# A decoder layer in split fp32: the set subtractions go from GpSimd to VectorE, and the merge gates' sigmoids stand one product behind their load

## The chip, the cores and the metric

The kernel runs on one core of a Trainium2 chip. TensorE multiplies matrices, VectorE, ScalarE and GpSimd work element by element, and the queue of SyncE (SP) issues nearly all DMAs. Each engine works through its own queue in order; semaphores tie the queues together. The metric is the device time of one execution in microseconds (us). In the profile PE is TensorE (PEld its weight loads), DVE VectorE, ACT ScalarE, POOL GpSimd and SP SyncE.

## The reference

One layer over 2048 rows of width 1024, float32:

```python
u = x * (1.0 + scale) + shift                    # scale, shift, gate from silu(c) @ w_ada
q, k, v, a_gate, p_in, p_gate, m_a, m_p = split(u @ w_in)
a = sliding_window_sink_attention(q, k, v, ...) * silu(a_gate)
a = a @ w_attn_proj
p = einsum('bsgc,gcd->bsgd', multiscale_causal_pool(p_in), w_pool_mix)
p = (p * pool_scale) * silu(p_gate)
p = p @ w_pool_proj
y = sigmoid(m_a) * a + sigmoid(m_p) * p
y = (y @ w_out) * (1.0 + gate)
x = layer_norm(DEEPNORM_ALPHA * x + y, ln_gain, ln_bias)
```

## The kernel before

**Products.** Every float32 operand is split in two: a high part (a cast to the multiplier's 32-bit type, on ScalarE) and a low part (operand minus high part, on VectorE or GpSimd). One block product is three passes of four matmuls, high by high, high by low, low by high: twelve matmuls of 128x512. These twelve are the kernel's unit of time, called a product or a tick below.

**Seven products for eight.** Two tiles of 128 weight columns by two column halves of 512 rows would be eight block products; a `Quad` does them with seven by a Strassen-Winograd scheme. It needs sums of weight blocks, made on GpSimd per quad (`sum1`, line 268; `mid`, 272 and 273; `late`, 277), and sums of the other operand's blocks. These latter, the *sets*, are named B11, T1, T2, B21, T3, B22, T4; they are made once per stage and then serve all quads of it. `pair_split` (lines 305 and 131: cast, then low part) splits a quad's weight blocks into `w_set` tiles, three times per quad.

**Where the sets come from.** `sums_to` (line 198) makes a later stage's sets aside of the running stage: it loads four blocks into two `spare` tiles of 128x1024 (`fetch`), then does four subtractions of 128x512 in place, one after the other (`sub`: T1, T2, T4, T3, each on the result of an earlier one), and stores each result to DRAM through SP. With the first load at tick 0, the subtractions are put at ticks 4, 5.5, 7 and 8.5 and their stores 2.5 ticks behind. There are 24 such sets of four: 4 in the first stage (there with a scaling of the loaded blocks ahead, so 3.5 ticks later), 8 in the second, and 12, one each 8 ticks, in the merge part. So 96 subtractions, on GpSimd, line 212, shown in the profile as line 56, GpSimd, `spare<-spare` (some use other tiles as room, `first_qs`, `second_qs`, `second_kk`). In the stage that uses them `set_steps` loads the sets again and splits them (`set_T` and `set_B` in the profile), between the products.

**Order.** `pe`, `act`, `dve`, `pool` and `sp` are engines whose instructions keep the program's order among themselves (line 56 is this wrapper); calls by `nc.` may be put elsewhere by the scheduling layer below. `ring` runs groups of two quads; after each product it calls `tick`, which runs what hooks and `defer` have put at that tick.

**Stages.** 0 to 260 us: modulation, first sets and the gates of half the rows; 260 to 605 attention of that half, with products filling it; 605 to 800 and 800 to 1193 the same for the other half; 1193 to 1560 the merge part: for each half the attention projection and the pool projection, four times two groups; then the output product and the norm.

**The merge gates.** In the merge part each product's result is multiplied by a sigmoid. `gates_ahead` (line 594) makes `ahead`, which `back` calls when a group starts and again two ticks later: it loads four gate tiles `g` for both quads together each time (SP), and applies the sigmoid on ScalarE (line 605). The result of product B21 (tick 2 for the first quad) is the first to use one, by lines 616, 625 and 627.

Of the kernel before, what the change touches and what calls it, by code (L numbers as in the profile page):

```python
# [14 lines left out]
AF = mybir.ActivationFunctionType  # L15
ALU = mybir.AluOpType
# [43 lines left out]
def kernel(  # L60
# [22 lines left out]
    nc = tc.nc  # L83
    pe, act, dve, pool, sp = (Ordered(tc, e) for e in (nc.tensor, nc.scalar, nc.vector, nc.gpsimd, nc.sync))
# [110 lines left out]
    def put(q, store, name, i, src):  # L195
        q.dma_start(store[name][i // 2, :, i % 2, :], src)

    def sums_to(ph, store, i, load, work=None, sums=True):

        b = []  # L200

        def x(r, c):
            return b[r][:, c * CH : (c + 1) * CH]

        def fetch():
            b.extend((ph.spare(), ph.spare()))
            b.reverse()
            for r in (1, 0):
                load(b[r], r)

        def sub(out, a, c):
            return lambda: pool.tensor_tensor(x(*out), x(*a), x(*c), ALU.subtract)

        todo = [(0, fetch)]
        if work:
            todo += [(3, lambda: work(b[0], 0)), (3.5, lambda: work(b[1], 1))]
        made = [("B11", (0, 0)), ("B21", (1, 0)), ("B22", (1, 1))] if work else []
        if work and not sums:
            made.insert(1, ("B12", (0, 1)))
        puts = [(5 + 0.6 * n, *x) for n, x in enumerate(made)]  # L220
        if sums:
            at = 7.5 if work else 4
            for out, a, c, name in (
                ((0, 1), (0, 1), (0, 0), "T1"),
                ((1, 1), (1, 1), (0, 1), "T2"),
                ((1, 0), (1, 0), (1, 1), "T4"),
                ((0, 0), (1, 1), (0, 0), "T3"),
            ):
                todo.append((at, sub(out, a, c)))
                puts.append((at + 2.5, name, out))  # L230
                at += 1.5
        for at, name, z in puts:
            todo.append((at, lambda name=name, z=z: put(sp, store, name, i, x(*z))))
        return sorted(todo, key=lambda t: t[0])
# [9 lines left out]
    class Quad:  # L244
# [7 lines left out]
        def load(self, ph, own, q=nc.sync, e=nc.gpsimd):  # L252
            self.w, self.a22 = ph.weights(), ph.last(own)
            x = self.w
            if len(self.srcs[0].shape) == 3:
                for dst, src, half in ((x[:, 2, :], 1, 0), (self.a22, 1, 1), (x[:, 0, :], 0, 0), (x[:, 3, :], 0, 1)):
                    q.dma_start(dst.rearrange("p (k q) -> p k q", k=4), self.srcs[src][:, 4 * half : 4 * half + 4, :])
                if e is not None:
                    self.sum1(e)
                return  # L260
            q.dma_start(x[:, 2, :], self.srcs[1][:, 0:CH])
            q.dma_start(self.a22, self.srcs[1][:, CH:])
            q.dma_start(x[:, 0::3, :], by_two(self.srcs[0]))
            if e is not None:
                self.sum1(e)
# [186 lines left out]
    def defer(ticks, f):  # L452
        due.append((now[0] + ticks, len(due), f))
# [143 lines left out]
    def gates_ahead(name, s, m, raw):  # L597
        g = {}

        def ahead(ph, turn):  # L600
            for mi, t in (((0, 0), (1, 1)), ((0, 1), (1, 0)))[turn]:
                x = g[mi, t] = ph.c("g")
                sp.dma_start(x, gates_d[name][s, m + mi, t])
                if raw:
                    nc.scalar.activation(x, x, AF.Sigmoid)

        return g, ahead

# [1036 lines left out]
```

## Time and profile before

| | |
|---|---|
| Median of 3 runs | 1693.99 us (1690.03 to 1697.75) |
| The profiled execution's own time | 1691.31 us |
| Its span, first to last instruction | 1689.5 us |
| TensorE busy | 1647.0 us, 97% of the span |
| VectorE, ScalarE, GpSimd busy | 1204.8, 1021.7, 995.3 us |
| Granted TensorE clock, mean | 0.996 |
| Merge part, 1193 to 1560 us: TensorE, VectorE, GpSimd busy | 359.11, 314.58, 218.58 of 367 us |
| DMA share in the merge part | 0.86 |

How to read the rows. A group row gives the line, the engine, the operation, the tiles (out, then in), shapes and count; behind the first bar the busy time in us and the mean of one in ns; behind the second the engine's idle time just ahead of these instructions and what ended it. A row in order of time gives start and length in us, then the same, with the idle time ahead in brackets. A row of waits gives who waited for whom: us in total, times, longest. A row of a stretch gives, from PE to POOL, busy us and in brackets the number of instructions, then the granted TensorE clock as a share of full speed, the busy share of the DMA engines and GB/s. The shown busy time of matmuls is modelled; their pace is read from the time of twelve in a row.

### The profile page before, as it was taken

The numbers are of one execution on the slowest core, as the hardware profiler recorded it, in microseconds if no ns is written. First come the engines' busy times: TensorE is split into PE (matmuls) and PEld (weight loads), VectorE is DVE, ScalarE is ACT, GpSimd is POOL, SyncE is SP. The second block draws the span as 40 slices with busy tenths as digits, with TensorE's granted clock in tenths as the row PEclk, the third lists the DMA queues.
The fourth block names the chain that finished last, engine by engine and source line by source line (L and its number), as shares of the span: only waits on it lengthen the run. The fifth ranks groups of instructions, "written<-read, shape, count | busy, mean of one in ns | idle before, by whom it ended". The sixth has DMA issues, their size and how long they took to land.

```text
span 1689.5 us, 24673 instructions
## 1 busy us (share of the span) xinstructions
PE 1647.0 (97%) x8058; PEld 1384.2 (82%) x8058; DVE 1204.8 (71%) x2140; ACT 1021.7 (60%) x2142; POOL 995.3 (59%) x734
## 2 busy tenths in 40 slices
PE   7999999999999999999999999999999999999997
PEld 6788888888888888888788888888878877888886
DVE  6955655776857657357467677675679997989877
ACT  4644547778777756334578777776546445645452
POOL 3343347586866838762376858587567667533442
PEclk9999999999999999999999999999999999999999
DMA  9688843333423468875542334223979797878443
GB/s 360 203 260 310 212 162 107 113 126 112 150 100 107 131 233 312 271 242 181 198 138 87 126 130 136 102 93 131 325 250 392 257 372 255 323 274 280 150 150 113
DMA packets 188850, 336.80 MB, mean 199 GB/s; under 512 B 18336, under 2 KB 44080, under 8 KB 188720
## 3 DMA queue, kind: packets, MB, share of 16 engines
q1 hardware_dynamic: 185600, 330.96, 57.2%
q10 hardware_dynamic: 3088, 4.23, 1.1%
q8 instruction: 64, 1.05, 0.2%
q14 instruction: 66, 0.54, 0.1%
q0 software_dynamic: 32, 0.02, 0.0%
HBM read 227.96 MB, written 110.33 MB: 200 GB/s over the span
## 4 chain that ended last, share of the span: by engine, by line
PE 67%; DVE 12%; DMA 7%; issue 5%; ACT 5%; POOL 4%; SPq 1%; POOLq 0%; DVEq 0%; ACTq 0%
PE mm L56 44%; PE lg L56 16%; PE pv L56 4%; PE pt L56 3%; DVE w_set L131 3%; DVE set_T L56 2%; DVE set_B L56 1%; ACT L L56 1%; DMA g<-ma_d 1%; DMA g<-mp_d 1%; POOL spare L56 1%; DVE w_set L56 1%; ACT w_set L56 1%; DVE wide L627 1%; DMA W<-in_win_dram 1%
## 5 line engine op out<-in xcount | busy, mean ns | idle before, releaser
L56 PE MATMUL mm<-set_B,w_set 128*128 128x512 f32 x2664 | 655.3, 393 | 2.2 <-DVE w_set L131 1.6
L56 PEld LDWEIGHTS mm<-set_B,w_set 128*128 128x128 f32 x2664 | 497.1, 189 | 106.2 <-DVE w_set L131 3.0
L56 PE MATMUL mm<-set_T,w_set 128*128 128x512 f32 x1824 | 454.3, 395 | 6.3 <-DVE mm L56 3.9
L56 PE MATMUL lg<-set_T,w_set 128*128 128x512 f32 x1704 | 412.0, 391 | 10.1 <-DVE w_set L131 5.7
L56 PEld LDWEIGHTS mm<-set_T,w_set 128*128 128x128 f32 x1824 | 335.9, 188 | 76.5 <-DVE mm L56 6.5
L56 PEld LDWEIGHTS lg<-set_T,w_set 128*128 128x128 f32 x1704 | 319.5, 188 | 81.1 <-DVE w_set L131 6.9
L131 DVE TENSOR_TENSOR w_set<-W,w_set 128x1024 fp32r<-128x1024 f32 x138 | 203.2, 1474 | 137.6 <-ACT w_set L305 124.1
L305 ACT CAST w_set<-W 128x1024 fp32r<-128x1024 f32 x138 | 144.8, 1050 | 215.4 <-PE mm L56 134.1
L56 POOL TENSOR_TENSOR w_set<-W,w_set 128x512 fp32r<-128x512 f32 x120 | 157.3, 1319 | 116.5 <-ACT w_set L56 114.6
L268 POOL TENSOR_TENSOR W<-W,A 128x512 f32<-128x512 f32 x46 | 73.0, 1586 | 233.3 <-DMA A<-in_win_dram 66.1
L56 DVE TENSOR_TENSOR o<-pv,o 64x128 f32<-64x128 f32 x256 | 72.1, 282 | 133.8 <-ACT o L56 127.4
L56 POOL TENSOR_TENSOR spare<-spare 128x512 f32<-128x512 f32 x68 | 127.8, 1882 | 27.1 <-DMA spare<-pin_B 10.3
L56 POOL TENSOR_TENSOR W<-W 128x512 f32<-128x512 f32 x82 | 108.3, 1335 | 53.2 <-DVE sm L56 29.5
L56 ACT ACTIVATE L<-L,nm 128x257 f32<-128x257 f32 (+1 forms) x256 | 127.2, 499 | 9.4 <-DVE nm L56 3.6
L277 POOL TENSOR_TENSOR W<-W 128x512 f32<-128x512 f32 x46 | 74.7, 1625 | 94.6 <-DVE w_set L131 87.0
L56 DVE CUSTOM_DVE_ANT_0 L<-lg,bt,nsink 128x256 f32<-128x256 f32 (+1 forms) x256 | 111.7, 473 | 20.3 <-PE lg L56 11.3
L56 ACT CAST w_set<-W 128x512 fp32r<-128x512 f32 (+1 forms) x164 | 100.3, 626 | 20.2 <-POOL W L56 15.0
L272 POOL TENSOR_TENSOR W<-W 128x512 f32<-128x512 f32 x44 | 72.7, 1655 | 65.1 <-DVE w_set L131 53.7
L56 ACT COPY o<-pv 64x256 f32<-64x256 f32 x128 | 47.3, 370 | 76.3 <-PE pv L56 75.0
L56 DVE TENSOR_TENSOR ptl<-pt,pth 128x512 fp32r<-128x512 f32 (+1 forms) x128 | 85.7, 670 | 1.3 <-ACT pth L56 1.0
L273 POOL TENSOR_TENSOR W<-W 128x512 f32<-128x512 f32 x44 | 71.9, 1635 | 20.6 <-DMA W<-in_win_dram 17.0
L56 ACT ACTIVATE L<-L,sm 128x256 f32<-128x256 f32 (+1 forms) x128 | 64.3, 502 | 31.5 <-DVE sm L56 31.2
(230 smaller groups left out, 2398.7 us busy)
## 6 DMA issues: line engine op xcount, KB each, us to landing
W<-in_win_dram SPq DMA_DIRECT2D x42, 512.0 KB, 5.8
W<-in_win_dram SPq DMA_DIRECT2D x42, 256.0 KB, 3.8
A<-in_win_dram SPq DMA_DIRECT2D x42, 256.0 KB, 5.1
ag_d<-sig SPq DMA_DIRECT2D x32, 256.0 KB, 5.9
pg_d<-sig SPq DMA_DIRECT2D x32, 256.0 KB, 4.2
pg<-pg_d SPq DMA_DIRECT2D x32, 256.0 KB, 3.2
pin_B<-fin SPq DMA_DIRECT2D x32, 256.0 KB, 2.0
ag<-ag_d SPq DMA_DIRECT2D x32, 256.0 KB, 3.0
```

The lines of the kernel that those rows point to most:

```text
L56: return lambda *args, **kw: self.tc.keep_in_program_order(op(*args, **kw))
L131: engine.tensor_tensor(dst, src, as32(hi), ALU.subtract)
L268: e.tensor_tensor(self.w[:, 1, :], self.w[:, 2, :], self.a22, ALU.add)
L272: e.tensor_tensor(x[:, 1, :], x[:, 1, :], x[:, 0, :], ALU.subtract)
L273: e.tensor_tensor(x[:, 2, :], x[:, 0, :], x[:, 2, :], ALU.subtract)
L277: e.tensor_tensor(x[:, 3, :], x[:, 3, :], x[:, 1, :], ALU.subtract)
L305: a.copy(by_two(hi), raw)
L627: nc.vector.tensor_tensor(dst, g, dst, ALU.add)
```

## The change

Two lines. The subtractions of `sums_to` are done by VectorE instead of GpSimd; their operands, their ticks and their stores stay. And `ahead` puts the sigmoid of a gate tile one tick behind the tile's load instead of right at it; the load stays.

```diff
         def sub(out, a, c):
-            return lambda: pool.tensor_tensor(x(*out), x(*a), x(*c), ALU.subtract)
+            return lambda: dve.tensor_tensor(x(*out), x(*a), x(*c), ALU.subtract)
...
                 x = g[mi, t] = ph.c("g")
                 sp.dma_start(x, gates_d[name][s, m + mi, t])
                 if raw:
-                    nc.scalar.activation(x, x, AF.Sigmoid)
+                    defer(1, lambda x=x: nc.scalar.activation(x, x, AF.Sigmoid))
```

TensorE's order stays as it was. On ScalarE, the start of the first merge group before: two casts of weight pairs (line 305), with the casts of sets and the sigmoids between them.

```order
L305 CAST w_set<-W 128x1024
L56 CAST set_T_566<-set_T_566 128x2x512
L351 COPY p_12871<-mm 128x512
L56 CAST set_B_565<-set_B_565 128x2x512
L305 CAST w_set<-W 128x1024
L56 CAST set_B_565<-set_B_565 128x2x512
L56 CAST set_T_567<-set_T_567 128x2x512 x2
L605 ACT_TABLE_LOAD
L605 ACTIVATE g<-g 128x512 x6
L305 CAST w_set<-W 128x1024
L605 ACTIVATE g<-g 128x512 x2
```

The same place now:

```order
L305 CAST w_set<-W 128x1024
L56 CAST set_T_566<-set_T_566 128x2x512
L351 COPY p_12867<-mm 128x512
L305 CAST w_set<-W 128x1024
L56 CAST set_B_565<-set_B_565 128x2x512
L56 CAST set_T_567<-set_T_567 128x2x512
L605 ACT_TABLE_LOAD
L605 ACTIVATE g<-g 128x512 x4
L56 CAST set_B_565<-set_B_565 128x2x512
L605 ACTIVATE g<-g 128x512 x4
L56 CAST set_T_567<-set_T_567 128x2x512
L305 CAST w_set<-W 128x1024
```

All eight sigmoids and four set casts now stand between the last two weight casts, where there were six sigmoids and three set casts; one set cast no longer stands ahead of the first of them. On VectorE, the same place before, from the split of the middle weight pair to that of the last (line 131):

```order
L131 TENSOR_TENSOR w_set<-W,w_set 128x1024
L56 TENSOR_TENSOR set_B_565<-set_B_565 128x2x512
L366 TENSOR_TENSOR mm<-lg,p_12871 128x512
L56 TENSOR_TENSOR set_T_567<-set_T_567 128x2x512 x2
L616 TENSOR_TENSOR wide_12869<-mm,g 128x512
L616 TENSOR_TENSOR wide_12911<-mm,g 128x512
L388 TENSOR_TENSOR p_12817<-lg,p_12817 128x512
L616 TENSOR_TENSOR wide_12945<-p_12817,g 128x512
L131 TENSOR_TENSOR w_set<-W,w_set 128x1024
```

And now, from the row ahead of that middle split, where one subtraction stands, to the last pair's set row:

```order
L56 TENSOR_TENSOR spare<-spare 128x512
L131 TENSOR_TENSOR w_set<-W,w_set 128x1024
L56 TENSOR_TENSOR set_B_565<-set_B_565 128x2x512
L56 TENSOR_TENSOR spare<-spare 128x512
L366 TENSOR_TENSOR mm<-lg,p_12867 128x512
L56 TENSOR_TENSOR spare<-spare 128x512
L56 TENSOR_TENSOR set_T_567<-set_T_567 128x2x512
L616 TENSOR_TENSOR wide_12865<-mm,g 128x512
L616 TENSOR_TENSOR wide_12911<-mm,g 128x512
L388 TENSOR_TENSOR p_12813<-lg,p_12813 128x512
L56 TENSOR_TENSOR set_B_565<-set_B_565 128x2x512
L616 TENSOR_TENSOR wide_12945<-p_12813,g 128x512
```

Behind these follow one more `set_T_567` row, one more row of line 616 and then the last pair's split; three subtractions and one product row more than before stand ahead of it. On GpSimd the subtractions are gone and the sums of the weight blocks follow each other directly.

## The prediction

> **What bounds the kernel now.** I read the page's first section, then busy time by stage, then who ended TensorE's waits.
>
> ```profile
> span 1689.5 us, 24673 instructions
> PE 1647.0 (97%) x8058; PEld 1384.2 (82%) x8058; DVE 1204.8 (71%) x2140; ACT 1021.7 (60%) x2142; POOL 995.3 (59%) x734
> ```
>
> The matmuls are busy for 97% of the span, so only about 42 us are open to any change. The next view cuts the span: the stage of the first subtractions (100 to 245), the second (650 to 750), the whole merge part (1193 to 1560), and three pieces of it.
>
> ```profile
> core 0: us, PE busy (x) PEld busy (x) DVE busy (x) ACT busy (x) POOL busy (x), PEclk, DMA share, GB/s
> 100.00:245.00 145.00, 145.00 (x724) 123.18 (x723) 84.70 (x100) 68.15 (x103) 55.15 (x36) 1.00 0.77 242
> 650.00:750.00 100.00, 100.00 (x443) 82.81 (x442) 51.94 (x43) 39.47 (x56) 79.16 (x54) 1.00 0.78 269
> 1193.00:1560.00 367.00, 359.11 (x1562) 293.63 (x1561) 314.58 (x286) 194.53 (x254) 218.58 (x123) 0.99 0.86 304
> 1243.28:1250.00 6.72, 6.72 (x19) 5.30 (x20) 5.10 (x6) 1.05 (x1) 2.76 (x2) 0.64 0.74 211
> 1281.00:1319.00 38.00, 38.00 (x169) 31.45 (x169) 37.97 (x30) 22.01 (x29) 27.98 (x14) 1.00 0.86 322
> 1357.00:1396.00 39.00, 37.42 (x164) 30.32 (x163) 38.26 (x30) 18.70 (x22) 30.89 (x16) 1.00 1.02 369
> ```
>
> In the first two stages TensorE never rests and VectorE rests for 60.3 of 145 and 48.1 of 100 us. In the merge part TensorE loses 367.00 - 359.11 = 7.9 us, and VectorE is full in two stretches (37.97 of 38, 38.26 of 39). TensorE's waits there:
>
> ```profile
> PE lg L56 <- DVE w_set L131: 4.0, 1, 4.0
> PE lg L56 <- DVE p L388: 1.8, 4, 0.9
> PE mm L56 <- DVE w_set L131: 1.2, 2, 1.0
> ```
>
> One wait holds half of it. In time order, and with two lines of the chain of waits beside it:
>
> ```profile
> 1237.28 1.98 PE L56 MATMUL lg<-set_T,w_set 128*128 128x512 f32 x8
> 1243.28 2.07 PE L56 MATMUL lg<-set_T,w_set 128*128 128x512 f32 x4 [4.02 <-DVE w_set L131]
> ```
>
> ```profile
> 1187.88 2.73 PE lg L56 x12
> 1245.35 4.12 PE mm L56 x12
> ```
>
> Twelve matmuls take 2.73 us at full clock (0.2275 each) and 4.12 after the wait, where the granted clock is 0.64. The 4 + 12 matmuls behind it take 2.07 + 4.12 = 6.19 us instead of 3.64: the place costs 4.0 of waiting and 2.55 of slow clock, **6.6 us** of all that the merge part loses. The other waits listed come to 3.0 us.
>
> **The change, part one: 96 subtractions from GpSimd to VectorE.** Durations alone and beside the other engine, from the lines in time order:
>
> ```profile
> 228.64 1.30 POOL L56 TENSOR_TENSOR spare<-spare 128x512 f32<-128x512 f32 x1
> 242.89 0.69 DVE L131 TENSOR_TENSOR w_set<-A,w_set 128x512 fp32r<-128x512 f32 x1 [0.54 <-ACT w_set L312]
> 1302.28 1.21 DVE L131 TENSOR_TENSOR w_set<-W,w_set 128x1024 fp32r<-128x1024 f32 x1
> 1304.55 2.31 DVE L131 TENSOR_TENSOR w_set<-W,w_set 128x1024 fp32r<-128x1024 f32 x1
> 1305.74 2.28 POOL L56 TENSOR_TENSOR spare<-spare 128x512 f32<-128x512 f32 x1
> ```
>
> A 128x512 subtraction of two SBUF tiles takes GpSimd 1.30 us alone and 2.28 beside VectorE; VectorE's 128x1024 takes 1.21 alone and 2.31 beside GpSimd. So a subtraction left on GpSimd can cost VectorE 2.31 - 1.21 = 1.10 us, and moved there costs it 0.69 (the same shape and operands as the w_set row) plus what it waits for the GpSimd work that stays. The Trainium skill, "SBUF — State Buffer", section "Who interferes with whom", says that a VectorE instruction with two SBUF inputs and a GpSimd instruction that reads SBUF exclude each other for a whole instruction; by it one meeting would cost VectorE up to GpSimd's 1.30 and 48 removed ones return at most 62 us rather than 53. The trace agrees in kind and is lower (1.10), so 1.10 is used.
>
> First stage, 16 subtractions: 16 x 0.69 = 11.0 us more for VectorE, covered by its 60.3 us of rest; second stage, 32: 22.1 us, covered by 48.1. Each is taken at 0; TensorE's waits there are nil, so nothing can be won, and without that cover each 0.69 ahead of a weight split would show. I keep -0 and +1 us for each. Their stores on SP come later with VectorE's queue, and one of them now stands just ahead of a weight load of the attention part; that is what the +1 is for.
>
> Merge part, 48 subtractions. The VectorE groups with two SBUF inputs, and GpSimd's subtractions:
>
> ```profile
> L131 DVE TENSOR_TENSOR w_set<-W,w_set 128x1024 fp32r<-128x1024 f32 x55 | 83.8, 1525 | 37.7 <-ACT w_set L305 37.7
> L56 DVE TENSOR_TENSOR set_T<-set_T 128x1024 fp32r<-128x1024 f32 x39 | 59.7, 1540 | 2.9 <-ACT set_T L56 2.9
> L56 DVE TENSOR_TENSOR set_B<-set_B 128x1024 fp32r<-128x1024 f32 x30 | 53.2, 1785 | 3.5 <-ACT set_B L56 3.5
> L627 DVE TENSOR_TENSOR wide<-g,wide 128x512 f32<-128x512 f32 x32 | 33.2, 1037 | 0.4
> L131 DVE TENSOR_TENSOR w_set<-A,w_set 128x512 fp32r<-128x512 f32 x20 | 22.5, 1146 | 0.3 <-ACT w_set L312 0.3
> L56 POOL TENSOR_TENSOR spare<-spare 128x512 f32<-128x512 f32 x48 | 94.7, 1977 | 21.7 <-DMA spare<-pin_B 10.3 <-DMA spare<-ain_B 8.2 <-DMA spare<-wo_B 2.2
> ```
>
> Over their times alone these groups lose 55 x 0.315 + 39 x 0.33 + 30 x 0.575 + 32 x 0.347 + 20 x 0.456 = 67.7 us. The subtractions are 94.7 of GpSimd's 218.58 us, so their share is 29.3 (ends: nothing, and 48 x 1.10 = 52.8; I take the share, as it comes from the whole part). VectorE gets 48 x 0.69 = 33.1, plus waiting: its 128x512 groups lose 0.39 each now, times the 57% of GpSimd's work that stays, 0.22 x 48 = 10.6. Net 33.1 + 10.6 - 29.3 = +14.4 us, in 367 us of which VectorE rests 52.4. Where it is full, 77 of the 367 us, the share is 3 us, and part of it is taken up by splits that stand products ahead of their use; I take **+1.0 us**. Ends: -3.0 (the other waits go, since GpSimd, with 95 us less, has the weight sums ready sooner) and +9.7 (four subtractions come every 8 products of 2.73 us, so 14 in those 77 us: 14 x 0.69, nothing returned).
>
> The wait for the loads moves too: VectorE's queue now stands still where GpSimd's did. The worst case:
>
> ```profile
> 1358.22 0.69 DVE L627 TENSOR_TENSOR wide<-g,wide 128x512 f32<-128x512 f32 x1
> 1358.83 2.37 POOL L56 TENSOR_TENSOR spare<-spare 128x512 f32<-128x512 f32 x1 [9.56 <-DMA spare<-pin_B]
> ```
>
> GpSimd waited 9.56 us, but VectorE comes to the same place of the program, ahead of the row at 1358.22, 0.6 us before the load was there; 0 to +2 us, taken as 0. Behind it would stand the set splits and the next weight split. On SP the stores waited for GpSimd:
>
> ```profile
> SPq L56 <- POOL spare L56: 34.7, 9, 12.7
> ```
>
> These 34.7 us go, and shorter ones for VectorE come, since GpSimd's subtractions also queued behind weight sums that waited for DMAs. A store that is some us late holds up loads behind it, but several us of landings are already queued (DMA share 0.86 over the part). Taken at 0, ends -1 and +2.
>
> **Part two: the sigmoids one product later.** ScalarE's queue before the long wait:
>
> ```profile
> 1226.56 1.05 ACT L305 CAST w_set<-W 128x1024 fp32r<-128x1024 f32 x1
> 1231.34 1.28 ACT L605 ACT_TABLE_LOAD   x1
> 1232.63 3.24 ACT L605 ACTIVATE g<-g 128x512 f32<-128x512 f32 x6
> 1235.78 1.04 ACT L305 CAST w_set<-W 128x1024 fp32r<-128x1024 f32 x1
> ```
>
> The cast at 1235.78 feeds the late split. In the new order one set cast (1.05) and two sigmoids (2 x 0.54) more stand between the two weight casts, while the first of these may start up to 1.05 earlier: the second ends 1.1 to 2.1 us later, at 1237.9 to 1239.0, against a product that starts at 1237.28. So the product starts 0.6 to 1.7 us late. What ended the wait, though, was the split on VectorE, which had been full for the 20 us before:
>
> ```profile
> 1222.70:1243.20 20.50, 16.55 (x73) 13.34 (x72) 20.45 (x16) 14.97 (x20) 14.10 (x8) 0.95 0.94 341
> ```
>
> ```profile
> L56 POOL TENSOR_TENSOR spare<-spare 128x512 f32<-128x512 f32 x5 | 11.2, 2250 | 0.1
> ```
>
> ```profile
> L131 DVE TENSOR_TENSOR w_set<-W,w_set 128x1024 fp32r<-128x1024 f32 x3 | 6.9, 2299 | 0.0
> L56 DVE TENSOR_TENSOR set_T<-set_T 128x1024 fp32r<-128x1024 f32 x4 | 6.4, 1618 | 0.7 <-ACT set_T L56 0.7
> L56 DVE TENSOR_TENSOR set_B<-set_B 128x1024 fp32r<-128x1024 f32 x2 | 4.0, 2016 | 0.0
> ```
>
> Here VectorE loses 3 x 1.09 + 4 x 0.41 + 2 x 0.81 = 6.5 us to GpSimd, of whose 16.1 us in these groups (3.6 and 1.3 in two weight-sum groups beside) the subtractions are 70%: 4.6 come back. By the new order it does one product row (0.69) and three subtractions (2.07) more ahead of that split: 1.8 us earlier in all. The wait becomes 2.2 us, in two pieces with matmuls between. Whether the clock then drops is open: 4.02 us were followed by 0.64, and the wait of 1.0 (in 1357 to 1396) by 1.00. I take half of the 2.55. Term: -1.8 - 1.3 = **-3.1 us**; ends -6.6 (all gone) and +5 (the split 2.8 later with nothing returned, and 2 us more at the slow clock).
>
> The Trainium skill, "TensorE: Matmul & The Clock Gate", section "HAM oscillation", tells to keep idle gaps under some 3.4 us; by it both pieces are harmless and the term would be -4.4 instead of -3.1. The trace agrees so far as it has one gap above that and a slow clock behind it.
>
> **Sum.** The profiled execution took 1691.31 us, its span 1689.5 and 1.8 around it. 1691.31 + 0 + 0 + 1.0 - 3.1 = 1689.2. The median of the runs shown, 1693.99, is 2.7 above that execution; with the same distance I forecast **1691.9 us**.
>
> **Rivals.** Half a per cent, 8.5 us, is about what a measurement of this kernel can tell from no change.
> - *VectorE becomes the bound* in the full stretches 1281 to 1319 and 1357 to 1396: GpSimd's remaining sums meet VectorE more often, nothing is returned, and 14 x 0.69 = 9.7 us go to TensorE, on the median's 1693.99: 1703.7, slower. It decides where the mean of the w_set rows stays near 1525 ns. For it: 38 of 38 us busy. Against: 0.69 against up to 1.10.
> - *The sigmoids stand in front of the weight cast* and the long wait grows to the +5 end: 1693.99 + 5 + 1.0 = 1700.0. For it: the order; against: VectorE, not ScalarE, ended that wait.
> - *The long wait dissolves*: -6.6, and -2.5 of the other waits as GpSimd's sums come sooner: 1693.99 - 9.1 = 1684.9. For it: five GpSimd subtractions stood beside the late splits. Against: nothing leaves VectorE's queue ahead of the split.
>
> **How the numbers follow.** Forecast 0.55, VectorE bound 0.20, sigmoids 0.12, dissolved 0.13. Slower by over 0.5% takes 0.17 of the second and a little of the third, 0.18; faster nearly all of the last, 0.11; the rest, 0.71, is within 0.5%. The range reaches from the dissolved case to the VectorE case, 1685 to 1704.
>
> **What would show it.** In the merge part GpSimd should have 75 instructions and some 110 us; the w_set, set_T and set_B means fall towards 1.4 us; VectorE's busy time rises by about 14 us; TensorE's longest wait is near 2 us, and the clock behind it tells which half of the 2.55 was right. In the first two stages TensorE stays at full. The forecast is wrong if a new wait over 3 us for w_set, set_T or a DMA appears on TensorE, or if PE's busy time changes in the attention parts, which the change does not touch.

## The result, and the profile after

The changed kernel took 1704.04 us (median of 7 runs, 1700.34 to 1707.04) against 1693.99 us (7 runs, 1690.03 to 1698.05). The ratio is 1.0053 with an interval of 1.0037 to 1.0068: slower by half a per cent, some 9 us (the two medians differ by 10.1 us), where 2 us faster was forecast. The profiled execution took 1700.34 us, 9.0 more than the one before. The page's first lines of the changed kernel, and then busy time by stage in the stretches shown of before (the last one is new; columns as before):

```profile
span 1698.6 us, 24603 instructions
PE 1651.7 (97%) x8058; PEld 1388.2 (82%) x8058; DVE 1229.3 (72%) x2236; ACT 1022.6 (60%) x2142; POOL 835.4 (49%) x638
```

```profile
100.00:245.00 145.00, 145.00 (x724) 123.26 (x723) 89.09 (x113) 68.24 (x103) 36.39 (x24) 1.00 0.77 241
650.00:750.00 100.00, 100.00 (x443) 82.81 (x442) 68.62 (x74) 39.84 (x56) 32.17 (x22) 1.00 0.79 272
1193.00:1560.00 367.00, 355.41 (x1527) 289.81 (x1526) 312.63 (x326) 192.71 (x250) 129.57 (x74) 0.98 0.84 298
1396.00:1407.50 11.50, 8.11 (x22) 5.76 (x21) 7.56 (x9) 6.52 (x11) 2.88 (x2) 0.70 0.49 187
```

In the first two stages TensorE is still full. The merge part has lost time: by 1560 us 1527 matmuls are recorded instead of 1562, and 35 x 0.2275 us is 8.0 of the 9.0 us. GpSimd's 218.58 us have become 129.57, and VectorE has done 326 instructions instead of 286 in less time than before. TensorE's waits in the merge part (up to 1570 us):

```profile
PE lg L56 <- DVE w_set L131: 4.0, 4, 2.0
PE mm L56 <- ACT set_B L56: 2.9, 2, 1.5
PE mm L56 <- DVE w_set L131: 2.1, 1, 2.1
PE mm L56 <- DVE set_B L56: 1.8, 1, 1.8
PE lg L56 <- ACT w_set L305: 0.6, 1, 0.6
```

The one wait of 4.02 us is gone. New are the waits for `set_B`, first for ScalarE's cast and then for VectorE's low part. Before, no wait named `set_B`. One place, on TensorE, ScalarE and VectorE in order of time (the first group of the second half's attention projection, which the expectations below call the sixth group):

```profile
1398.31 1.21 PE L56 MATMUL mm<-set_B,w_set 128*128 128x512 f32 x4 [1.54 <-ACT set_B L56]
1401.36 2.93 PE L56 MATMUL mm<-set_B,w_set 128*128 128x512 f32 x6 [1.84 <-DVE set_B L56]
```

```profile
1395.13 2.18 ACT L605 ACTIVATE g<-g 128x512 f32<-128x512 f32 x4
1397.22 1.03 ACT L56 CAST set_B<-set_B 128x1024 fp32r<-128x1024 f32 x1
1398.16 2.19 ACT L605 ACTIVATE g<-g 128x512 f32<-128x512 f32 x4
```

```profile
1398.38 0.71 DVE L616 TENSOR_TENSOR wide<-p,g 128x512 f32<-128x512 f32 x1
1399.02 2.29 DVE L56 TENSOR_TENSOR set_B<-set_B 128x1024 fp32r<-128x1024 f32 x1
```

The second cast of `set_B` stands behind four sigmoids (2.18 us). The product that needs it waits 1.54 us; the cast ends at 1398.25, but VectorE has a result to multiply by its gate first (1398.38) and starts the low part only at 1399.02; that takes 2.29 us, against 1.21 us for this shape alone, and TensorE waits another 1.84. The clock falls behind it, by the stretches of the changed kernel:

```profile
1396.00:1400.70 4.70, 1.97 (x8) 0.97 (x6) 4.70 (x6) 4.70 (x9) 2.88 (x2) 1.00 1.04 399
1400.70:1407.50 6.80, 6.14 (x14) 4.79 (x15) 2.86 (x4) 1.82 (x3) 0.00 (x0) 0.50 0.11 40
```

14 matmuls take 6.14 us where 14 x 0.2275 = 3.2 would do, so the place costs 1.54 + 1.84 + 2.9 = 6.3 us. It is as dear as the long wait that went.

### The profile page after: what moved, and what is told of

Its sections match the earlier page's. It is cut to its first block, busy times and chain, and to the rows that moved or that the text cites. A ratio compares the mean times of both kernels' runs of the same rounds, so it can differ in the third digit from the quotient of the medians.

```text
span 1698.6 us, 24603 instructions
## 1 busy us (share of the span) xinstructions
PE 1651.7 (97%) x8058; PEld 1388.2 (82%) x8058; DVE 1229.3 (72%) x2236; ACT 1022.6 (60%) x2142; POOL 835.4 (49%) x638
## 4 chain that ended last, share of the span: by engine, by line
PE 76%; DVE 8%; DMA 6%; ACT 5%; issue 3%; POOL 2%; SPq 1%; POOLq 0%; DVEq 0%; ACTq 0%
PE mm L56 49%; PE lg L56 19%; PE pt L56 4%; PE pv L56 4%; DMA set_T<-ain_T 2%; DVE set_T L56 1%; DMA g<-mp_d 1%; DVE w_set L131 1%; ACT L L56 1%; DMA g<-ma_d 1%; ACT g L605 1%; DMA A<-in_win_dram 1%; DVE w_set L56 1%; ACT w_set L56 1%; DVE L L56 1%
## 5 line engine op out<-in xcount | busy, mean ns | idle before, releaser
L131 DVE TENSOR_TENSOR w_set<-W,w_set 128x1024 fp32r<-128x1024 f32 x138 | 176.7, 1282 | 111.8 <-ACT w_set L305 103.2
L268 POOL TENSOR_TENSOR W<-W,A 128x512 f32<-128x512 f32 x46 | 77.6, 1687 | 340.5 <-DMA A<-in_win_dram 67.3
L277 POOL TENSOR_TENSOR W<-W 128x512 f32<-128x512 f32 x46 | 74.0, 1609 | 147.9 <-DVE w_set L131 129.4
L56 POOL TENSOR_TENSOR W<-W 128x512 f32<-128x512 f32 x82 | 108.3, 1335 | 53.1 <-DVE sm L56 31.0
L272 POOL TENSOR_TENSOR W<-W 128x512 f32<-128x512 f32 x44 | 75.0, 1706 | 100.3 <-DVE w_set L131 91.3
L273 POOL TENSOR_TENSOR W<-W 128x512 f32<-128x512 f32 x44 | 75.4, 1713 | 34.3 <-DMA W<-in_win_dram 28.1
L56 PE MATMUL lg<-kk,qs 128*128 128x256 f32 (+1 forms) x512 | 80.6, 279 | 0.9 <-DMA kk<-k_end_d 0.9
```

The lines of the kernel that those rows point to most:

```text
L56: return lambda *args, **kw: self.tc.keep_in_program_order(op(*args, **kw))
L131: engine.tensor_tensor(dst, src, as32(hi), ALU.subtract)
L268: e.tensor_tensor(self.w[:, 1, :], self.w[:, 2, :], self.a22, ALU.add)
L272: e.tensor_tensor(x[:, 1, :], x[:, 1, :], x[:, 0, :], ALU.subtract)
L273: e.tensor_tensor(x[:, 2, :], x[:, 0, :], x[:, 2, :], ALU.subtract)
L277: e.tensor_tensor(x[:, 3, :], x[:, 3, :], x[:, 1, :], ALU.subtract)
```

## The experiments

All ratios are to the kernel before, run beside it on the same chip.

**Each half alone, and each half's halves.** The subtractions alone (the sigmoids stay at their load):

```diff
-                    defer(1, lambda x=x: nc.scalar.activation(x, x, AF.Sigmoid))
+                    nc.scalar.activation(x, x, AF.Sigmoid)
```

> All 96 subtractions on VectorE, the sigmoids at their old place. Theory by places: of the changed kernel's loss the fifth group of 14 products in the merge part (1349.9 to 1393.9 us, +3.7 us; TensorE waits 1.52 and 2.12 us for weight splits that have a subtraction ahead of them on VectorE) belongs to the subtractions, the sixth (+5.3) and ninth (+3.5) to the sigmoids. Then this kernel takes 3.7 us more than the kernel before, 1697.7, or 1694 if the first group's gain of 3.5 belongs to the subtractions too; the waits of TensorE for set_B are gone. Rival, VectorE is the bound throughout: about 10 us more, 1704, with the loss still in the fifth, sixth and ninth groups.

Measured: 1689.14 us, ratio 0.9963 (0.9949 to 0.9976), faster by 6.3 us, with an interval clear of no change. Neither theory had that. Of TensorE's waits in the merge part (us in total, times, longest) there remain:

```profile
PE lg L56 <- DVE p L388: 1.6, 1, 1.6
PE mm L56 <- DVE w_set L131: 1.0, 2, 0.9
```

The long wait is gone. In the stretch ahead of it, 1222.7 to 1243.2 us, the three splits of weight pairs took 2299 ns each on average before, as the prediction shows; now:

```profile
L131 DVE TENSOR_TENSOR w_set<-W,w_set 128x1024 fp32r<-128x1024 f32 x3 | 3.6, 1216 | 0.0
```

This profile turned out to be the best of several (see *A wait that goes with the execution*).

The sigmoids alone (against the kernel before):

```diff
-                    nc.scalar.activation(x, x, AF.Sigmoid)
+                    defer(1, lambda x=x: nc.scalar.activation(x, x, AF.Sigmoid))
```

> Only the sigmoids are moved, the subtractions stay on GpSimd. On ScalarE the second cast of set_B (and in places the second of set_T) now stands behind three or four sigmoids in each group. Theory by places: the sixth and ninth groups lose 5.3 + 3.5 us, so 1694 + 8.8 = 1702.8, or 1699.3 if the first group's gain of 3.5 belongs to the sigmoids; TensorE waits for set_B in two pieces of 1.5 to 1.8 us near 1396 and the granted clock halves behind them. Rival, VectorE is the bound: within 1 us of the kernel before, or up to 3.5 us faster, and no wait for set_B above 1 us.

Measured: 1709.61 us, ratio 1.0081 (1.0062 to 1.0100), 13.7 us slower, more than either theory said. The waits of the merge part:

```profile
PE mm L56 <- DVE set_B L56: 5.8, 2, 3.2
PE mm L56 <- DVE w_set L131: 5.1, 3, 4.7
PE lg L56 <- DVE w_set L131: 4.5, 3, 2.2
PE lg L56 <- DVE p L388: 2.8, 2, 1.8
PE mm L56 <- ACT set_B L56: 1.5, 1, 1.5
```

`set_B` holds 7.3 us of them. So the change is a gain of 0.37% and a loss of 0.81%. The two add up to 0.44%, near the 0.53% measured for both.

The subtractions of the first two stages alone:

```diff
-    def sums_to(ph, store, i, load, work=None, sums=True):
+    def sums_to(ph, store, i, load, work=None, sums=True, eng=dve):
...
-            return lambda: pool.tensor_tensor(x(*out), x(*a), x(*c), ALU.subtract)
+            return lambda: eng.tensor_tensor(x(*out), x(*a), x(*c), ALU.subtract)
...
-            for offset, f in sums_to(ph, raw, i, load_raw(raw, i)):
+            for offset, f in sums_to(ph, raw, i, load_raw(raw, i), eng=pool):
```

> Only the 48 subtractions of the first two stages go to VectorE; the 48 of the merge part stay on GpSimd and the sigmoids at their old place. My prediction's terms for these two stages were 0 each, with ends of 0 and +1: 1694 (at most 1696), with no new wait of TensorE before 1193 us. Rival, later stores on SP delay the loads of the attention or merge part: 2 us or more above the kernel before, with a DMA among the releasers of TensorE.

Measured: 1696.63 us, ratio 1.0002 (0.9988 to 1.0016). They change nothing; the gain is that of the 48 in the merge part. Only the attention gates' sigmoids moved, with all subtractions on VectorE:

```diff
-                if raw:
+                if raw and name == "ma":
                     defer(1, lambda x=x: nc.scalar.activation(x, x, AF.Sigmoid))
+                elif raw:
+                    nc.scalar.activation(x, x, AF.Sigmoid)
```

> As the changed kernel, but only the sigmoids of the attention gates are moved; those of the pool gates are at their old place. Theory by places: the loss of 3.5 us in the ninth group, a group of pool gates in which no subtraction is left, goes, and the sixth group (attention gates) keeps its 5.3: 1704.0 - 3.5 = 1700.5. Rival, VectorE is the bound: no change from the changed kernel, 1704, since no subtraction is moved.

Measured: 1701.99 us, ratio 1.0030 (1.0014 to 1.0047). Above the subtractions alone that is 0.67% of the changed kernel's 0.90%, so the groups with attention gates carry much of the loss. The interval overlaps that of the changed kernel, so a cost of the pool gates' sigmoids is not shown.

**What in the sigmoids' move costs.** `act` is ScalarE with this wrapper:

```python
class Ordered:
    ...
    def __getattr__(self, name):
        op = getattr(self.engine, name)
        return lambda *args, **kw: self.tc.keep_in_program_order(op(*args, **kw))
```

It pins an instruction behind the one that was *written last* for its engine, and behind no other. `split` casts sets through `act`; the sigmoids are written through `nc.scalar` and are not pinned themselves. At their old place the instruction written next is no set cast. Put one tick later they are the last thing written ahead of a tick's hooks, so three set casts in each two groups (the first halves of B22 and T4, the second of B11) are pinned behind a sigmoid. The next kernel takes these pins away:

```diff
-                    defer(1, lambda x=x: nc.scalar.activation(x, x, AF.Sigmoid))
+                    def gate(x=x):
+                        nc.scalar.activation(x, x, AF.Sigmoid)
+                        free[0] = True
+                    defer(1, gate)
...
-            act.copy(t[:, :, 0, :], raw(name, half))
+            (nc.scalar if free[0] else act).copy(t[:, :, 0, :], raw(name, half))
+            free[0] = False
```

> As the changed kernel, but a set's cast that is written right behind a moved sigmoid is no longer pinned behind it. ScalarE, VectorE, GpSimd and TensorE then have the same order as with the subtractions alone; only some stores on SP differ. Theory: the loss comes from that pin and not from the later place of the sigmoids: 1694.9 x 0.9963 = 1688.6. Rival: sigmoids written a product later cost time by themselves (results later on VectorE): 1704.

Measured: 1687.06 us, ratio 0.9951 (0.9939 to 0.9963). The loss is gone. In the merge part ScalarE's and VectorE's queues are then row for row those of the subtractions alone: in the source the sigmoids are written a product later, in the queue they are not. So the sigmoids' move changed the order of a few casts, and that alone cost the time. With `free` used for all casts but T4's:

```diff
-            (nc.scalar if free[0] else act).copy(t[:, :, 0, :], raw(name, half))
+            (nc.scalar if free[0] and name != "T4" else act).copy(t[:, :, 0, :], raw(name, half))
```

> As the changed kernel, but of the pinned casts only those of set_B are free; the one of set_T (T4, used last in a group) stays behind a moved sigmoid. Theory: the late set_B casts are the loss, since TensorE's new waits name set_B: 1689, at most 1691. Rival: the set_T cast counts as much: 1696 or more, with waits of TensorE for set_T or w_set.

Measured: 1690.03 us, ratio 0.9965 (0.9952 to 0.9977): the `set_B` casts carry nearly all of it, as TensorE's waits said. The interval overlaps that of all casts freed, so a cost of T4's cast is not shown. Two products later instead of one, with the subtractions on VectorE:

```diff
-                    defer(1, lambda x=x: nc.scalar.activation(x, x, AF.Sigmoid))
+                    defer(2, lambda x=x: nc.scalar.activation(x, x, AF.Sigmoid))
```

> Subtractions on VectorE, sigmoids written two products behind their load instead of one. Behind the second product the next instruction written for ScalarE is no set cast, so nothing is pinned, and the four computing engines have the order that they have with the subtractions alone. Theory, the pin alone costs: 1687 to 1690, the time of the run with freed casts. Rival, later sigmoids: worse than one product, above 1704.

Measured: 1688.43 us, ratio 0.9957 (0.9944 to 0.9970). A longer delay costs nothing, since behind the second product no cast is written next: here too ScalarE's and VectorE's queues in the merge part are those of the subtractions alone.

**Why the subtractions gain.** Three kernels with the subtractions on VectorE and the sigmoids at their load, and idle work on GpSimd at each of the 48 places (a tile of zeros for itself):

```diff
                 todo.append((at, sub(out, a, c)))
+                if idle is not None:
+                    todo.append((at, lambda: [pool.tensor_tensor(idle, idle, idle, ALU.subtract) for _ in range(2)]))
```

> Subtractions on VectorE and sigmoids at the old place, plus idle work on GpSimd at the place of each of the 48 subtractions of the merge part: two 128x256 subtractions of a tile of zeros that nobody else uses. Every other instruction stands as with the subtractions alone. Theory, meetings: what the subtractions alone gained came from GpSimd's reads that no longer keep VectorE waiting; VectorE gets back some 32 us of longer instructions, and the time goes back to that of the kernel before or above, 1695 to 1700. Rival, queues: the gain came from weight sums that no longer stand on GpSimd behind subtractions waiting for their loads (21.7 us); the idle ones wait for nothing, so 1689 to 1691.

Measured: 1708.32 us, ratio 1.0072 (1.0060 to 1.0085). With every queue but GpSimd's as in the kernel with the subtractions alone, the time rises by 1.09%, 18 us, and the long wait is back (4.7 us, in the second row; the 6.4 us in the first stand near 1387 us):

```profile
PE mm L56 <- DVE w_set L131: 6.6, 2, 6.4
PE lg L56 <- DVE w_set L131: 6.2, 3, 4.7
PE lg L56 <- DVE p L390: 4.6, 3, 1.9
```

In the stretch ahead of the long wait VectorE is full again, 21.65 of 21.80 us; the cast that the late split needs had ended at 1240.3 us, and the split came at 1246.1:

```profile
1225.80:1247.60 21.80, 17.29 (x77) 13.97 (x75) 21.65 (x20) 15.74 (x21) 17.80 (x13) 0.94 0.92 335
```

The same with `pool.memset(idle, 0.0)`, twice at each place:

> As the run with idle subtractions on GpSimd, but with two 128x256 memsets each, which read nothing. Theory, meetings by reading: VectorE's instructions keep their times of the run with the subtractions alone, 1689. Rival: any work of GpSimd costs as much, by its writes or by holding up the weight sums behind it: the same time as with the idle subtractions.

Measured: 1685.54 us, ratio 0.9945 (0.9933 to 0.9956). A memset took 312 ns there, so the 94 in the merge part's stretch filled GpSimd for 29 us against 108 of the idle subtractions. Seven at each place make the two alike:

```diff
-                    todo.append((at, lambda: [pool.memset(idle, 0.0) for _ in range(2)]))
+                    todo.append((at, lambda: [pool.memset(idle, 0.0) for _ in range(7)]))
```

> As the run with idle memsets, but seven of them (128x256, 0.312 us each in that run) at the place of each subtraction of the merge part, so that GpSimd is as long busy with them (48 x 7 x 0.312 = 105 us) as it was with the idle subtractions (108 us). Theory, meetings by reading: VectorE's w_set rows stay near 1.34 us and the time near that of the subtractions alone, 1689 (at most 1692, for weight sums that stand 2.2 us behind memsets). Rival, occupancy of GpSimd: late weight sums cost as much as with the idle subtractions, 1705 or more, with ScalarE's casts waiting for GpSimd ahead of TensorE's waits.

Measured: 1690.43 us, ratio 0.9962 (0.9950 to 0.9974), the ratio of the subtractions alone. Three group rows of the merge part, first with the idle subtractions, then with seven memsets:

```profile
L56 POOL TENSOR_TENSOR idle<-idle 128x256 f32<-128x256 f32 x94 | 108.1, 1150 | 5.0
L56 DVE TENSOR_TENSOR spare<-spare 128x512 f32<-128x512 f32 x48 | 49.2, 1024 | 0.1
L56 DVE TENSOR_TENSOR set_B<-set_B 128x1024 fp32r<-128x1024 f32 x28 | 46.7, 1685 | 0.2 <-ACT set_B L56 0.2
```

```profile
L56 POOL MEMSET idle<- 128x256 f32 x329 | 102.6, 312 | 16.4
L56 DVE TENSOR_TENSOR spare<-spare 128x512 f32<-128x512 f32 x48 | 44.2, 920 | 0.6 <-DMA spare<-ain_B 0.5
L56 DVE TENSOR_TENSOR set_B<-set_B 128x1024 fp32r<-128x1024 f32 x30 | 44.0, 1484 | 0.3 <-ACT set_B L56 0.2
```

GpSimd is busy for as long in the merge part (226.12 us with the idle subtractions, 221.15 with seven memsets), and its weight sums stand behind nearly as much idle work; what differs is that the memsets read nothing, and VectorE's rows with two SBUF inputs are shorter. So it is GpSimd's reads that cost, by VectorE's queue, and not its occupancy. Some of the 18 us may still come by later weight sums: ScalarE's casts waited for them 42.5 us with the idle subtractions, 33.0 without, and 22.3 with the memsets, where 9.4 more were spent waiting for the memsets themselves.

Is VectorE's own load then harmless? Each subtraction of the merge part twice on VectorE, none on GpSimd:

```diff
-                todo.append((at, sub(out, a, c)))
+                for _ in range(times):
+                    todo.append((at, sub(out, a, c)))
...
-            for offset, f in sums_to(ph, raw, i, load_raw(raw, i)):
+            for offset, f in sums_to(ph, raw, i, load_raw(raw, i), times=2):
```

> Subtractions on VectorE, sigmoids at the old place, and each of the 48 subtractions of the merge part done twice in place (the second run of one works on the result of the first, so the stored sums have other values). VectorE's load grows by 48 x 0.88 = 42 us on 328 of 367 us, with no more reads of GpSimd. Theory, meetings: a subtraction added on VectorE costs less than one added on GpSimd, since it holds up nobody else: below the 1708 of the idle subtractions, about 1695, as VectorE has some 39 us of rest and splits late by a row or two where it is full. Rival, VectorE's load alone decides: 1708 or more, as 42 us are more than the idle subtractions brought back.

Measured: 1704.15 us, ratio 1.0052 (1.0039 to 1.0064), against 1695 expected. It stays below the idle subtractions, but the 48 more cost 0.89%, 15 us. TensorE's wait for splits in the merge part, and the group row of the subtractions:

```profile
PE lg L56 <- DVE w_set L131: 15.7, 9, 3.4
```

```profile
L56 DVE TENSOR_TENSOR spare<-spare 128x512 f32<-128x512 f32 x96 | 83.0, 868 | 1.0
```

VectorE takes 48 subtractions at no loss, but not 96.

**A wait that goes with the execution.** The kernel with the subtractions alone, profiled once more without an edit:

> The subtractions alone once more, for a second profile. The wait for w_set near 1367 us was 0.87 us in its first profile, but 4.9 and 5.2 in those of the two runs with freed casts, whose computing engines have the same or nearly the same order. If that wait goes with the execution and not with the order, it can be 4 to 5 us here too; if it goes with the order of the stores on SP, it is again below 1.5.

This execution took 1691.74 us, and its wait for `w_set` near 1367 us was 4.8 us instead of 0.9:

```profile
1368.77 1.19 PE L56 MATMUL mm<-set_B,w_set 128*128 128x512 f32 x4 [0.87 <-DVE w_set L131]
1372.56 2.08 PE L56 MATMUL mm<-set_B,w_set 128*128 128x512 f32 x4 [4.78 <-DVE w_set L131]
```

GpSimd's first weight sum there and what VectorE did beside it, in the first profile and then in the second:

```profile
1359.94 4.70 POOL L268 TENSOR_TENSOR W<-W,A 128x512 f32<-128x512 f32 x1 [17.80 <-DVE set_T L56]
1359.86 0.68 DVE L625 TENSOR_TENSOR g<-p,g 128x512 f32<-128x512 f32 x1
1361.66 0.68 DVE L56 TENSOR_TENSOR spare<-spare 128x512 f32<-128x512 f32 x1
```

```profile
1358.69 2.29 POOL L268 TENSOR_TENSOR W<-W,A 128x512 f32<-128x512 f32 x1 [16.67 <-DVE p L388]
1359.75 1.78 DVE L625 TENSOR_TENSOR g<-p,g 128x512 f32<-128x512 f32 x1
1364.86 1.78 DVE L56 TENSOR_TENSOR spare<-spare 128x512 f32<-128x512 f32 x1
```

The same instructions meet in the same place. In the first execution GpSimd's sum starts 0.08 us behind VectorE's row; it takes 4.70 us, and VectorE's rows keep their 0.68. In the second it starts 1.06 us ahead of that row, and VectorE's rows take 1.78 each. Of four such rows in a line (4 x 1.10 = 4.4 us) the weight split ahead of TensorE is late.

The first profile, though, is the exception. The same product waits for the same split in all the runs whose VectorE order in the merge part is that of the subtractions alone: 4.9 us with all casts freed, 4.2 with the sigmoids two products late, 3.7 and 3.1 with two and seven memsets; with the `set_B` casts freed, nearly the same order, it is 5.2. Behind each of these the next twelve matmuls took 3.5 to 4.9 us instead of 2.9. In the kernel before the wait was 1.0 us, and 1.1 with only the first stages' subtractions moved. So in six of seven profiles the subtractions come with a wait of 3 to 5 us there, and my theory by places, which had given this stretch to them, is not refuted by the one with 0.9. The stretch is not theirs alone: with only the sigmoids moved the same product waited 4.75 us. So part of what the long wait cost is paid again here.

## Why the prediction was wrong, by its own steps

- **First two stages, 0 each:** right. TensorE's rows are full, and the subtractions there alone gave 1.0002.
- **Merge part, VectorE's net load, +14.4 us:** too high. With the subtractions alone (first profile) the stretch of 367 us shows 327.61 - 314.58 = +13.0, but it holds 1605 recorded matmuls instead of 1562, so more work. The stretch and two of its group rows:

```profile
1193.00:1560.00 367.00, 364.38 (x1605) 300.55 (x1603) 327.61 (x343) 201.31 (x262) 135.85 (x78) 1.00 0.86 309
```

```profile
L56 DVE TENSOR_TENSOR spare<-spare 128x512 f32<-128x512 f32 x48 | 42.1, 877 | 0.7 <-DMA spare<-ain_B 0.5
L131 DVE TENSOR_TENSOR w_set<-W,w_set 128x1024 fp32r<-128x1024 f32 x57 | 76.5, 1342 | 32.3 <-ACT w_set L305 32.3
```

  Over the same work, from 1193 us to the end, the run with only the first stages' subtractions moved (its merge part is that of before), and then the two profiles of the subtractions alone:

```profile
1193.00:1712.00 519.00, 481.71 (x2105) 394.83 (x2103) 420.87 (x433) 255.07 (x346) 270.43 (x160) 0.99 0.71 252
1193.00:1712.00 519.00, 479.06 (x2108) 394.89 (x2106) 425.59 (x482) 255.94 (x346) 184.67 (x112) 0.99 0.71 252
1193.00:1712.00 519.00, 481.27 (x2105) 396.15 (x2103) 421.57 (x481) 256.06 (x346) 181.97 (x112) 0.98 0.71 251
```

  That is +4.7 and +0.7 us. The subtractions themselves took 42.1 us (33.1 + 10.6 = 43.7 expected), so the term that was mis-sized is the return: more than the 29.3 us came back from the other rows. The `w_set` mean fell from 1525 to 1342 ns.
- **Its price in time, +1.0 (ends -3.0 to +9.7):** wrong; it was -6.3 (interval -8.6 to -4.1). The failing step is the one that spread the load evenly over the full stretches, "the share is 3 us". What cost TensorE is a run of meetings ahead of the one split that comes last, as at 1238 us. I had seen that and put it into the other term as 1.8 us earlier. With the subtractions alone the 4.02 us and the 2.55 of slow clock there were gone in both profiles, which is the case that I had called *the long wait dissolves* and given 0.13. Its 1684.9 us were not reached (1689.14), since a wait near 1370 us mostly came in its place.
- **The sigmoids, -3.1 (ends -6.6 to +5):** wrong; alone they cost 13.7 us (10.5 to 16.9). The failing step: I followed the *weight* casts between which the sigmoids stand ("one set cast and two sigmoids more"), for one group. The order shown in the section on the change has the row that mattered, the second `set_B_565` cast behind `ACTIVATE g x4`. I costed neither who needs that cast (product B22) nor that it recurs in later groups: in the changed kernel the place of the long wait keeps 1.32 + 0.60 us of waits at full clock, where 6.6 us were lost, and the place near 1398 us loses 6.3 us.
- **Half of the 2.55 us of slow clock:** at the place of the long wait all of it was saved (the clock is 1.00 from 1230 to 1244 us of the changed kernel), but the clock fell at other places. The Trainium skill, "TensorE: Matmul & The Clock Gate", section "HAM oscillation", asks for no idle gaps above some 3.4 us. The trace differs: 1.54 and 1.84 us, with four matmuls between, were followed by 6.8 us at 0.50. The measurement decides.
- **SP, 0:** no wait of TensorE in the merge part ended with a DMA, so no cost was seen, but not for my reason. The stores' wait, 34.7 us before, did not shorten in the changed kernel's merge part:

```profile
SPq L56 <- DVE spare L56: 39.7, 14, 12.7
```

- **The rivals.** *VectorE becomes the bound* gave 1703.7 us, nearly the number measured, but its sign did not come: it decides where the `w_set` mean stays near 1525 ns, and it fell to 1342 with the subtractions alone, where the time fell, and to 1278 in the changed kernel, where the time rose. Twice the subtractions show that this bound is real, one dose further on. *The sigmoids in front of the weight cast* had the right engine and reason; it was the set cast, in several groups, and so 13.7 instead of 5 us.
- **The signs:** GpSimd's count was right (74 for 75), its 129.57 us above the 110 foretold: the mean weight sum rose from 1.70 to 1.78 us instead of falling. That they now meet VectorE's subtractions is likely, but not shown. The signs named for a wrong forecast did not come: no new wait is over 3 us, and TensorE's busy time in the attention parts is as before (339.94 and 389.01 us, now 339.86 and 388.05); the loss came in waits of 2.1 us and less, and in the clock behind them. That the longest was near 2 us as forecast is luck: it stands at 1372 us, for another split.

## What to carry to other kernels

When an instruction moves in an engine's queue, list what now stands behind it and follow each of these to the product that needs it, in every group and not only in the one with the longest wait; a helper that pins an instruction behind whatever was written last turns a delay of one thing into an order of another. Judge work moved between VectorE and GpSimd not by the sum of their busy times but by which instructions read SBUF together ahead of the split that comes last; and change two such things apart, since here a gain of 0.37% was hidden behind a loss of 0.81%. The subtractions on VectorE with the sigmoids left alone, or with the casts unpinned, beat both kernels (0.9963 and 0.9951).

## What was not expected of the hardware

- GpSimd memsets cost VectorE nothing measurable (0.9962 with 103 us of them) where subtractions of the same occupancy cost 18 us. The Trainium skill, "SBUF — State Buffer", section "Who interferes with whom", says that a VectorE instruction with two SBUF inputs contends with a GpSimd instruction that reads SBUF and not with one that only writes it; the runs agree.
- Which of the two engines loses at a meeting changed between two executions of one kernel (4.70 and 0.68 us, or 2.29 and 1.78), and moved one wait of TensorE from 0.9 to 4.8 us. One profile of such a place is one draw, and here the first was the rare one of seven.
- In the changed kernel the clock fell to 0.50 for 3.4 us behind a single wait of 1.96 us (TensorE in order of time, then the stretch behind):

```profile
1530.24 5.24 PE L56 MATMUL lg<-set_T,w_set 128*128 128x512 f32 x13 [1.96 <-DVE w_set L131]
```

```profile
1530.40:1533.80 3.40, 3.40 (x9) 2.63 (x10) 3.40 (x6) 1.51 (x2) 0.00 (x0) 0.50 0.85 321
```

  Nine matmuls took 3.40 us there instead of 2.05. The wait of 2.2 us in the run with the sigmoids alone was followed by full clock; what tells them apart stays open.
